# A decoder trunk on one core: seven more side steps in the second branch, an earlier and divided dt chain, and the added halves one pair of blocks per step

## Chip, core and metric

The kernel runs on one core of a Trainium2 chip, as one launch. The metric is the device time of one execution in microseconds (us), and a kernel's time is the median of its runs. The core has a matrix engine (TensorE; PE in the profile, PEld for its weight loads), a vector engine (VectorE, DVE), an engine for functions of single elements (ScalarE, ACT), a general engine (GpSimd, POOL) and SyncE (SP), whose queue issues all of this kernel's transfers.

## What is computed

One layer of a decoder, for 512 positions of width 1024, in float32. A normed input `u` is multiplied by one wide matrix `w_in`; its columns feed three mixers (windowed attention in three groups of six heads, causal pooling, a state space scan, SSD), whose outputs are gated, added and projected; a gated convolution network and two more norms follow.

```python
u = rmsnorm(x, ln1_g)
q, k, v, pool_in, z, xbc, dt_raw, gate_pre = jnp.split(u @ w_in, split_idx, axis=-1)
y_a = dilated_attention_mixer(q, k, v, rel_bias) @ w_a
y_b = pool_mixer(pool_in, pool_w, pool_scale) @ w_b
y_c = ssd_mixer(z, xbc, dt_raw, ...) @ w_c
gates = sigmoid(gate_pre + b_gate).reshape(b, s, 3, D_MODEL)
x = x + (gates[:, :, 0] * y_a + gates[:, :, 1] * y_b + gates[:, :, 2] * y_c) @ w_o
x = x + conv_ffn(rmsnorm(x, ln2_g), ...)
out = rmsnorm(x, final_g)
# inside ssd_mixer
dt = jax.nn.softplus(dt_raw + dt_bias)
A = -jnp.exp(a_log)
a_cs = jnp.cumsum(dt * A, ...)      # per chunk of 128 positions
```

The change lies in the stretch of the second branch (`w_b`), the first half of its gates and the products for `v` of the second and third attention groups.

## The kernel before, in words

**Products.** Each float32 operand is split into a high part and a low part (names ending in `h` and `l`), and a product is three products of the parts. `mm3` (L230) writes them: first high weights with high inputs, then high with low, then low with high. A chunk of 128 output columns over a depth of 1024 is 3 x 8 = 24 matmuls of 128x512 into one bank of PSUM, the matrix engine's result memory (`chunk_a`; tile `pa`).

**Jobs.** The program is a list of jobs; each takes one block of weights (256 columns, so two chunks, in `jobs_a`). While job n runs, `prepare` has already written the low part of job n+1 (`lows`, L211, VectorE), asks for the high part of job n+2 (`cast`, L191, ScalarE, in two halves, each at one of the next two steps) and issues the load of job n+3 (`fetch`, L179, SyncE). The engines' own orders are the orders in which the kernel's code emits instructions (a manual schedule for PE, ACT, DVE and POOL); each engine works through its queue in order. There are two raw buffers, three for high parts, two for low parts, four PSUM banks for chunks (`mm`) and four for everything else (`sm`).

**Steps.** Work beside the big products is put between them by `step()`. A step lets every generator in `running` go on to its next `yield`, then takes one item off `waiting`, starts it and moves it to `running`. In the second branch, the gates and the q and k products a step follows each chunk; in the v pair (`sevens`) one follows each product. Chunks of the last q and k jobs (`qk_jobs`, group 2) are already cut into two runs of 12 matmuls, with a step between.

**Attention items.** `attend(0)` puts twelve items (three pairs of heads, two banks of blocks, two heads) and one for statistics on `waiting`. An item computes scores `ps` for both heads of a pair if it is the first of them (L651), adds the bias (L658 to L665), takes the maximum (L661, L669) and the exponential (L672, ScalarE); two steps later it transposes the probabilities (`pt`, L678) and copies them to `sb` (L679, by VectorE for the even head and by ScalarE for the odd one); for the odd head, one step later still, come the products with v (`po`, L690), and after a pair's last bank their copy (L696, ScalarE).

**dt chain.** `ssd_prep` is one item of the same list, put in at place 5. It loads small vectors (first step), prepares dtx and an exponential (second), and in its third step runs 22 short instructions on VectorE one after another, a rational series for the logarithm (L845 to L855). Two steps later come four small matmuls (`pcs`, L859 to L862), then copies and exponentials, and one step on, four transposes (`pact`), two copies (`acst`, `east`) and their stores (`ad`, `ed`).

**Added halves.** The v columns of groups 1 and 2 are made with seven products in place of eight (`v_pair`, `sevens`), which take sums of quarters of the normed rows. The rows lie in eight blocks; `sums_of_u(p)` handles pair p of them. It adds high and low part of two blocks (`uf`, L388), next step forms four quarter sums `sa` and `sb` (L306 to L309), next step casts them (`sah`, `sbh`, ScalarE), next step subtracts (`sal`, `sbl`, L315 and L316, VectorE). The second product of `sevens` (the job `three`) reads `sbh` and `sbl` of all four pairs; the first (`one`) reads none. Beside the low part of their weights, `one`, `three` and `two` each form a difference of weight blocks on VectorE (L321).

In `program`, the four generators start ahead of the last job of the second branch, pairs 0 and 1 at its first step and pairs 2 and 3 one step later:

```python
yield Call(lambda: running.extend(after(p // 2, sums_of_u(p)) for p in range(4)))
```

Gate chunks are evacuated by a sigmoid (ScalarE, L1043) and multiplied into `yo` (VectorE, L1045). Sigmoid and exponential need different function tables on ScalarE (ACT_TABLE_LOAD).

Of the kernel before, what the change touches and what calls it, by code (L numbers as in the profile page):

```python
# [16 lines left out]
P = 128  # L17
# [66 lines left out]
def trunk(ctx: ExitStack, tc, out, x, rel_bias, ln1_g, w_in, b_gate, w_a, pool_w, pool_scale, w_b,  # L84
# [40 lines left out]
    waiting, running = [], []  # L125
# [19 lines left out]
    def step():  # L145
        flush()
        for it in list(running):
            try:
                next(it)
            except StopIteration:  # L150
                running.remove(it)
        if waiting:
            it = iter(waiting.pop(0))
            running.append(it)
            try:
                next(it)
            except StopIteration:
                running.remove(it)

    def after(n, it):  # L160
        for _ in range(n):
            yield
        yield from it
# [60 lines left out]
    def mm3(ps, wh, wl, xh, xl, ks, first=True, last=True, flip=False):  # L224

        n, total = 0, 3 * len(ks)
        for a, b in ((wh, xh), (wh, xl), (wl, xh)):
            for k in ks:
                l, r = (b(k), a(k)) if flip else (a(k), b(k))
                pe.matmul(ps, l, r, start=first and n == 0, stop=last and n == total - 1)  # L230
                n += 1

    def chunk_a(ps, ws, j, xh, xl, ks, lo=0, hi=S, k0=0):
        wh, wl = ws
        mm3(ps[:, lo:hi], lambda k: wh[:, k0 + k, j * P:(j + 1) * P],
            lambda k: wl[:, k0 + k, j * P:(j + 1) * P],
            lambda k: xh(k)[:, lo:hi], lambda k: xl(k)[:, lo:hi], ks)

    def jobs_a(w, c0, count, xh, xl, nk, evac, width=256):

        per = width // P
        for i in range(0, count, per):
            def body(ws, i=i):
                for j in range(per):
                    ps = MM("pa")
                    chunk_a(ps, ws, j, xh, xl, range(nk))
                    evac(i + j, ps)
                    if nk > 4 or j % 2:
                        step()
            yield Job([wsrc(w, 0, nk, c0 + i * P, c0 + i * P + width)], nk, width, body)  # L250
# [132 lines left out]
    def sums_of_u(p):  # L383

        f = []
        for k in (2 * p, 2 * p + 1):
            f.append(T("uf"))
            dve.tensor_tensor(f[-1], uh[:, k, :].bitcast(F32), ul[:, k, :].bitcast(F32), OP.add)  # L388
        yield
        yield from sums_of(*f, T("sah", F32R), T("sal", F32R),  # L390
                           lambda j, h, l: US.__setitem__((j, p), (h, l)))
# [210 lines left out]
    def qk_jobs(g):  # L602
        for i in range(3):
            def body(ws, i=i):
                for j, which in enumerate("qk"):
                    ps = MM("pqk")
                    if g == 2 and i >= 3 - MORE:

                        wh, wl = ws
                        for k0 in (0, 4):  # L610
                            mm3(ps, lambda k: wh[:, k, j * P:(j + 1) * P],
                                lambda k: wl[:, k, j * P:(j + 1) * P], uhk, ulk, range(k0, k0 + 4),
                                k0 == 0, k0 == 4)
                            if k0 == 0:
                                step()
                    else:
                        chunk_a(ps, ws, j, uhk, ulk, range(KD))
                    t = T(f"{which}{g}")
                    if which == "q":
                        act.mul(grouped(t, g), blocked(ps, g), 0.125)  # L620
                    else:
                        dve.tensor_copy(plain(t, g), perm(ps, g))
                    QK[which, g, i] = t
                    step()
            cq, ck = C_Q + 384 * g + i * P, C_K + 384 * g + i * P
            yield Job([wsrc(w_in, 0, KD, cq, cq + P), wsrc(w_in, 0, KD, ck, ck + P)], KD, 256, body)
# [131 lines left out]
    DP, YB = {}, {}  # L758
# [64 lines left out]
    def ssd_prep():  # L823

        f = lambda nme: cst.setdefault(nme, cpool.tile([P, n16], F32, name=nme))
        b16 = cpool.tile([P, 2, SH], F32, name="b16")
        for i, src in enumerate((ssd_dt_bias, ssd_a_log)):
            sp.dma_start(b16[:, i, :], src[0].partition_broadcast(P))

        dr, gr = T("dr"), T("gr")  # L830
        sp.dma_start(dr[:8, S - 2:], ssd_d[0].rearrange("(c h) -> c h", h=2))
        sp.dma_start(gr[:8, :P], ssd_norm_w[0].rearrange("(c p) -> c p", p=P))
        yield
        dve.tensor_copy(dr[:8, :P].rearrange("p (h d) -> p h d", h=2),
                        dr[:8, S - 2:].unsqueeze(2).to_broadcast([8, 2, DH]))
        dgc = cst["dgc"] = cpool.tile([P, 16], F32, name="dgc")
        v4 = lambda t: t.rearrange("p (a b) -> p a b", a=4)
        bc = lambda i: b16[:, i, :].unsqueeze(1).to_broadcast([P, 4, SH])
        xx, t, u, s, zz, dtv, a = (f(nme) for nme in ("dtx", "dtt", "dtu", "dts", "dtz", "dtv", "dta"))
        dve.tensor_tensor(v4(xx), dtr, bc(0), OP.add)  # L840
        dve.scalar_tensor_tensor(t, xx, -1.0, xx, OP.mult, OP.max)
        act.activation(t, t, AF.Exp, scale=-1.0)
        act.activation(b16[:, 1, :], b16[:, 1, :], AF.Exp)
        yield
        dve.tensor_scalar(u, t, 2.0, None, OP.add)  # L845
        dve.reciprocal(u, u)
        dve.tensor_mul(s, t, u)
        dve.tensor_mul(zz, s, s)
        dve.tensor_scalar(u, zz, 2.0 / 17, 2.0 / 15, OP.mult, OP.add)
        for d in (13, 11, 9, 7, 5, 3, 1):  # L850
            dve.tensor_mul(u, u, zz)
            dve.tensor_scalar(u, u, 2.0 / d, None, OP.add)
        dve.tensor_mul(u, u, s)
        dve.scalar_tensor_tensor(dtv, xx, 0.0, u, OP.max, OP.add)
        dve.scalar_tensor_tensor(v4(a), v4(dtv), -1.0, bc(1), OP.mult, OP.mult)  # L855
        yield
        yield
        ps = SM("pcs")
        pe.matmul(ps[:, :n16], tri, a, start=True, stop=True)  # L859
        pe.matmul(ps[:, n16:2 * n16], ones, a, start=True, stop=True)  # L860
        for i, r in enumerate((dr, gr)):
            pe.transpose(ps[:, 2 * n16 + 8 * i:2 * n16 + 8 * i + 8], r[:8, :P], eye[:8, :8])  # L862
        dve.tensor_copy(dgc, ps[:, 2 * n16:2 * n16 + 16])
        acs, tot, dec = (f(nme) for nme in ("acs", "tot", "dec"))
        dve.tensor_copy(acs, ps[:, :n16])
        dve.tensor_copy(tot, ps[:, n16:2 * n16])
        dve.tensor_tensor(dec, tot, acs, OP.subtract)
        act.activation(dec, dec, AF.Exp)
        act.activation(tot, tot, AF.Exp)
        yield  # L870
        pt = SM("pact")
        for c in range(4):
            pe.transpose(pt[:SH, c * P:(c + 1) * P], acs[:, c * SH:(c + 1) * SH], eye)
        at, et = T("acst"), T("east")
        dve.tensor_copy(at[:SH], pt[:SH])
        ad = cst["ad"] = dram.tile([SH, S], F32, name="ad")
        sp.dma_start(ad, at[:SH])
        act.activation(et[:SH], pt[:SH], AF.Exp)
        ed = cst["ed"] = dram.tile([SH, S], F32, name="ed")
        sp.dma_start(ed, et[:SH])  # L880
# [165 lines left out]

        return jobs_a(w_in, C_GATE + b * D + lo * P, hi - lo, uhk, ulk, KD, evac)

    def branch_jobs(b, w, parts, nk, last=False):
        def evac(m, ps):  # L1050
            if b == 1:
                MG[m] = T("yo")
                act.copy(MG[m], ps)
                return
            s = SG[b, m]
            dve.tensor_tensor(s, s, ps, OP.mult)
            (dve if last else pool).tensor_tensor(MG[m], MG[m], s, OP.add)
            if last:
                h, l = T("mgh", F32R), T("mgl", F32R)
                act.copy(h, MG[m])  # L1060
                dve.tensor_sub(l, MG[m], h.bitcast(F32))
                MH[m] = (h, l)

        return jobs_a(w, 0, 8, lambda k: parts[k][0], lambda k: parts[k][1], nk, evac,
                      width=256 if nk > 4 else 512)


    X1 = {}
# [319 lines left out]
    def program():  # L1388
# [3 lines left out]
        yield from qk_jobs(0)  # L1392
        yield from pool_out_job()
        yield Call(lambda: attend(0))
        yield Call(lambda: waiting.insert(5, ssd_prep()))
        for i, job in enumerate(branch_jobs(1, w_b, YB, 8)):
            if i == 3:
                yield Call(lambda: running.extend(after(p // 2, sums_of_u(p)) for p in range(4)))
            yield job
        load, pair = v_pair()  # L1400
        yield Call(load)
# [238 lines left out]
```

## Time and profile before

| what | value |
|---|---|
| runs of the kernel before | 1058.33, 1058.52, 1058.95 us; median 1058.52 |
| the profiled execution | 1059.66 us, of which 1057.6 us are the span from first to last instruction |
| mean granted clock of TensorE | 0.992 |
| busy: PE / PEld / DVE / ACT / POOL | 1039.9 / 866.4 / 642.2 / 477.7 / 137.9 us |
| second branch, four gate chunks (122.5 to 215.5 us) | 93.0 us: PE 87.2, DVE 54.7, ACT 46.5 busy, clock 0.93 |
| v pair (215.5 to 248.7 us) | 33.2 us: PE 33.2, DVE 28.5, ACT 18.4 busy, clock 1.00 |
| one chunk of 24 matmuls | about 5.4 us |

The profile names an instruction by engine, line, operation and tiles (out<-in), and a line can be that of a helper: L230 is `mm3`, whatever it works for. Times are from the span's start. "PEclk" is the share of full clock granted to TensorE, "[x <-Y]" the idle time before an instruction and what ended it, "x8" a merged run of eight.

### The profile page before, as it was taken

Reading aid. Unit: us, or ns where it says so; the run is one execution under the profiler, and the core shown is the slowest. Engines: PE = TensorE matmul, PEld = TensorE weight load, DVE = VectorE, ACT = ScalarE, POOL = GpSimd, SP = SyncE. Lnnn points to the kernel's source line nnn. Section 1 sums busy time; section 2 is a strip of 40 time slices with the busy share of each in tenths; the row PEclk is TensorE's granted clock in tenths of the full one; section 3 lists DMA queues with packets and bytes.
Section 4 is the critical chain, followed back from the end, with each engine's and each line's share of the span. In section 5 each row is a group of like instructions: output and inputs, shape, how many; then the busy total and the mean of one; then the engine's idle time right before and its main releaser. Section 6 shows DMA issues by size and latency. Waiting matters only on the chain.

```text
span 1057.6 us, 13100 instructions
## 1 busy us (share of the span) xinstructions
PE 1039.9 (98%) x5220; PEld 866.4 (82%) x5220; DVE 642.2 (61%) x867; ACT 477.7 (45%) x761; POOL 137.9 (13%) x118
## 2 busy tenths in 40 slices
PE   8999999799999999999999999999999999999997
PEld 8998888598888887788887888898888888878886
DVE  5553536776256556666577955766776656556545
ACT  6432542763384363566564423544444443433331
POOL 1770000000000001100135500001111111110110
PEclk9999999799999999999999999999999999999999
DMA  8454321125422346432244336643233232361332
GB/s 258 137 133 131 115 81 30 33 56 142 142 80 80 80 105 154 129 110 81 80 118 113 121 118 217 203 161 120 80 95 105 85 115 80 120 239 61 115 103 80
DMA packets 119787, 121.80 MB, mean 115 GB/s; under 512 B 5523, under 2 KB 101590, under 8 KB 119727
## 3 DMA queue, kind: packets, MB, share of 16 engines
q1 hardware_dynamic: 119727, 120.98, 37.5%
q8 instruction: 41, 0.67, 0.3%
q14 instruction: 19, 0.16, 0.0%
HBM read 115.07 MB, written 4.32 MB: 113 GB/s over the span
## 4 chain that ended last, share of the span: by engine, by line
PE 92%; DVE 3%; DMA 2%; ACT 2%; issue 0%; SPq 0%; DVEq 0%; ACTq 0%
PE pa L230 33%; PE pu L230 22%; PE pb L230 17%; PE pqk L230 9%; PE pa L1500 2%; PE p L230 2%; PE ps L651 1%; PE ppw L230 1%; PE po L690 1%; PE pt L678 1%; DMA al<-ad 1%; DMA raw<-in_w_in_dram 1%; DMA raw<-in_ffn_w_up_dram 1%; PE py L948 1%; PE pyo L954 1%; ACT wh L191 0%
## 5 line engine op out<-in xcount | busy, mean ns | idle before, releaser
L211 DVE TENSOR_TENSOR wl<-raw,wh 128x2048 fp32r<-128x2048 f32 (+3 forms) x95 | 218.5, 2300 | 89.3 <-ACT wh L191 53.6
L191 ACT CAST wh<-raw 128x1024 fp32r<-128x1024 f32 (+3 forms) x188 | 189.9, 1026 | 66.2 <-DVE raw L321 21.5
L230 PE MATMUL pa<-uh,wh 128*128 128x512 f32 x384 | 100.7, 405 | 0.0
L1158 DVE SCALAR_TENSOR_TENSOR hc<-pu,fcol,hc 128x510 f32<-128x510 f32 x88 | 65.8, 748 | 51.1 <-ACT hc L1155 49.5
L230 PE MATMUL pa<-ul,wh 128*128 128x512 f32 x384 | 95.2, 390 | 0.0
L230 PE MATMUL pa<-uh,wl 128*128 128x512 f32 x384 | 95.0, 390 | 0.0
L230 PEld LDWEIGHTS pa<-ul,wh 128*128 128x128 f32 x384 | 72.4, 189 | 15.4
L230 PEld LDWEIGHTS pa<-uh,wl 128*128 128x128 f32 x384 | 72.0, 188 | 15.3 <-DVE wl L211 0.3
L230 PEld LDWEIGHTS pa<-uh,wh 128*128 128x128 f32 x384 | 71.1, 191 | 16.2 <-issue 1.6
L230 PE MATMUL pu<-uh,wh 128*128 128x512 f32 (+1 forms) x352 | 83.7, 380 | 0.5 <-ACT uh L436 0.5
L230 PE MATMUL pu<-uh,wl 128*128 128x512 f32 (+1 forms) x352 | 83.5, 380 | 0.0
L230 PE MATMUL pu<-ul,wh 128*128 128x512 f32 (+1 forms) x352 | 83.5, 380 | 0.0
L230 PEld LDWEIGHTS pu<-uh,wh 128*128 128x128 f32 x352 | 64.1, 188 | 13.1 <-ACT uh L436 0.7
L230 PEld LDWEIGHTS pu<-ul,wh 128*128 128x128 f32 x352 | 64.2, 188 | 12.5
L230 PEld LDWEIGHTS pu<-uh,wl 128*128 128x128 f32 x352 | 64.2, 188 | 12.4
L1155 ACT ACTIVATE hc<-pu,fcol,fcol 128x512 f32<-128x512 f32 x40 | 31.2, 780 | 75.6 <-PE pu L230 75.3
L1163 POOL TENSOR_TENSOR hc<-hc 128x512 f32<-128x512 f32 x22 | 31.5, 1431 | 223.8 <-DVE hc L1158 169.3
L927 POOL TENSOR_TENSOR xd<-xc,dec 128x512 f32<-128x512 f32 x6 | 6.4, 1063 | 371.4 <-DVE xc L918 352.8
L672 ACT ACTIVATE sb<-sb,nm 128x128 f32<-128x128 f32 (+1 forms) x72 | 30.1, 419 | 29.3 <-DVE nm L669 18.1
L230 PE MATMUL pqk<-uh,wh 128*128 128x512 f32 x144 | 36.9, 394 | 0.0
L230 PE MATMUL pqk<-ul,wh 128*128 128x512 f32 x144 | 36.3, 390 | 0.0
L230 PE MATMUL pqk<-uh,wl 128*128 128x512 f32 x144 | 36.3, 390 | 0.0
(345 smaller groups left out, 1739.5 us busy)
## 6 DMA issues: line engine op xcount, KB each, us to landing
raw<-in_w_in_dram SPq DMA_DIRECT2D x25, 1024.0 KB
raw<-in_ffn_w_up_dram SPq DMA_DIRECT2D x22, 1024.0 KB
raw<-in_w_in_dram SPq DMA_DIRECT2D x20, 512.0 KB
raw<-in_ffn_w_down_dram SPq DMA_DIRECT2D x10, 1024.0 KB
raw<-in_w_o_dram SPq DMA_DIRECT2D x8, 1024.0 KB
raw<-in_w_b_dram SPq DMA_DIRECT2D x4, 1024.0 KB
al<-ad SPq DMA_DIRECT2D x16, 256.0 KB
raw<-in_w_c_dram SPq DMA_DIRECT2D x4, 1024.0 KB
```

The costliest lines, as they stand in the source:

```text
L191: act.copy(job.high[:, :, o], job.raw[:, :, o])
L211: (eng or dve).tensor_tensor(l[:, :, o], job.raw[:, :, o], h[:, :, o].bitcast(F32), OP.subtract)
L230: pe.matmul(ps, l, r, start=first and n == 0, stop=last and n == total - 1)
L651: pe.matmul(pss[i][:, o:o + w * P], q[r, n * P:(n + 1) * P], k[r, kb * P:(kb + w) * P], start=True, stop=True)
L672: act.activation(sb[:, off:off + w * P], sb[:, off:off + w * P], AF.Exp, bias=nm[:, n, h:h + 1], accum_out=ls[:, n, h:h + 1])
L678: pe.transpose(pt[:, o:o + P], sb[:, o:o + P], eye)
L690: pe.matmul(po[DH * hh:DH * hh + DH, n * P:(n + 1) * P], V[g, kb + i][:, (2 * c + hh) * DH:(2 * c + hh + 1) * DH], probs[2 * c + hh, nb][: ...
L948: pe.matmul(py[DH * i:DH * i + DH, j * P:(j + 1) * P], xc[:, o:o + DH], als[j // 2][:, lo:lo + P], start=True, stop=True)
L1155: act.activation(t, ps, AF.Identity, bias=ff["c1"][:, ff["b"] + m:ff["b"] + m + 1], scale=fw(2, m))
L1158: dve.scalar_tensor_tensor(t[:, sh:], ps[:, :S - sh], fw(k, m), t[:, sh:], OP.mult, OP.add)
L1163: pool.tensor_tensor(a, a, t, OP.mult)
L1500: pe.matmul(first[2 * n + j][:, lo:hi], a[:, k, j * P:(j + 1) * P], b[:, k, lo:hi], start=a is wh and b is uh and k == 0, stop=a is wl and ...
```

## The change

Three edits, no instruction of arithmetic added or taken away.

- Chunks 0 to 6 of the second branch are computed by a new `chunk_a2`: depth blocks 0 to 3 (12 matmuls), a step, depth blocks 4 to 7, into the same bank. `qk_jobs` calls the same function in place of its own copy of that code.
- `ssd_prep` goes into the list at place 3, two items further up, and a `yield` ahead of divisor 9 cuts the dt chain into two steps.
- The generators of the added halves start one pair per step (`after(p + 1, ...)`): pair 0 a step later than before, pairs 1, 2 and 3 each one step after the one before it.

```diff
+    def chunk_a2(ps, ws, j, xh, xl):
+
+        wh, wl = ws
+        for k0 in (0, 4):
+            mm3(ps, lambda k: wh[:, k, j * P:(j + 1) * P], lambda k: wl[:, k, j * P:(j + 1) * P],
+                xh, xl, range(k0, k0 + 4), k0 == 0, k0 == 4)
+            if k0 == 0:
+                step()
+
-    def jobs_a(w, c0, count, xh, xl, nk, evac, width=256):
+    def jobs_a(w, c0, count, xh, xl, nk, evac, width=256, more=()):
...
-                    chunk_a(ps, ws, j, xh, xl, range(nk))
+                    if i + j in more:
+                        chunk_a2(ps, ws, j, xh, xl)
+                    else:
+                        chunk_a(ps, ws, j, xh, xl, range(nk))
...
         for d in (13, 11, 9, 7, 5, 3, 1):
+            if d == 9:
+                yield
             dve.tensor_mul(u, u, zz)
...
-        yield Call(lambda: waiting.insert(5, ssd_prep()))
-        for i, job in enumerate(branch_jobs(1, w_b, YB, 8)):
+        yield Call(lambda: waiting.insert(3, ssd_prep()))
+        for i, job in enumerate(branch_jobs(1, w_b, YB, 8, more=range(7))):
             if i == 3:
-                yield Call(lambda: running.extend(after(p // 2, sums_of_u(p)) for p in range(4)))
+                yield Call(lambda: running.extend(after(p + 1, sums_of_u(p)) for p in range(4)))
             yield job
```

More of the change, by code (lines that the diff above doesn't have):

```diff
@@ L607, in body @@
                     if g == 2 and i >= 3 - MORE:
[L609 to L615, printed above, removed]
+                        chunk_a2(ps, ws, j, uhk, ulk)
                     else:
@@ L1047, in gate_jobs, with branch_jobs @@
         return jobs_a(w_in, C_GATE + b * D + lo * P, hi - lo, uhk, ulk, KD, evac)
-    def branch_jobs(b, w, parts, nk, last=False):
+    def branch_jobs(b, w, parts, nk, last=False, more=()):
         def evac(m, ps):
@@ L1064, in branch_jobs @@
         return jobs_a(w, 0, 8, lambda k: parts[k][0], lambda k: parts[k][1], nk, evac,
-                      width=256 if nk > 4 else 512)
+                      width=256 if nk > 4 else 512, more=more)
     X1 = {}
```

## The prediction, as it was made

> **What bounds the kernel now.** I read the page's busy times first, then its clock row, then TensorE's waits, then the timeline around the longest.
>
> ```profile
> PE 1039.9 (98%) x5220; PEld 866.4 (82%) x5220; DVE 642.2 (61%) x867; ACT 477.7 (45%) x761; POOL 137.9 (13%) x118
> ...
> PEclk9999999799999999999999999999999999999999
> ```
>
> TensorE is busy for 98% of the span, so only what stops or slows it can be won. The change moves work and leaves every matmul in place. One slice of the clock row is below 9: the eighth, 185 to 211 us. TensorE's waits between 100 and 260 us are two, both in that slice:
>
> ```profile
> PE po L690 <- ACT sb L679: 4.3, 1, 4.3
> PE ps L651 <- DVE tot L866: 1.5, 1, 1.5
> ```
>
> What the slice costs, the timeline of TensorE's weight loads tells, because the same train of work runs twice: the products of a head pair (po), three transposes (pt), a score block (ps), one chunk of 24 matmuls. First undisturbed, then in the bad place:
>
> ```profile
> 153.30 0.85 PEld L690 LDWEIGHTS po<-sb,v 128*64 128x64 f32 x16 [0.35 <-issue]
> ...
> 161.23 0.48 PEld L678 LDWEIGHTS pt<-eye,sb 128*128 128x128 f32 x3
> ```
> ```profile
> 187.31 0.19 PEld L690 LDWEIGHTS po<-sb,v 128*64 128x64 f32 x2
> 192.05 1.57 PEld L690 LDWEIGHTS po<-sb,v 128*64 128x64 f32 x14 [4.54 <-ACT sb L679]
> ...
> 206.68 0.53 PEld L873 LDWEIGHTS pact<-eye,acs 128*16 128x16 f32 x4
> ```
>
> 161.23 - 153.30 = 7.93 us against 206.68 - 187.31 = 19.37 us: **11.4 us are lost here**, 5.8 of them as waits, the rest because the clock is halved. The table by stretches shows that (columns: us, then PE, PEld, DVE, ACT, POOL busy, then PEclk):
>
> ```profile
> 186.35:189.76 3.41, 1.40 (x10) 0.99 (x8) 2.74 (x3) 3.38 (x6) 0.00 (x0) 1.00 0.17 18
> 189.76:193.17 3.41, 1.12 (x10) 1.12 (x12) 3.34 (x12) 3.39 (x6) 0.00 (x0) 0.50 0.60 215
> ...
> 200.00:203.41 3.41, 3.41 (x9) 2.64 (x8) 3.38 (x5) 2.34 (x7) 0.00 (x0) 0.50 0.00 0
> 203.41:206.82 3.41, 3.41 (x16) 2.72 (x15) 1.83 (x2) 0.84 (x1) 0.00 (x0) 1.00 0.00 0
> ```
>
> The clock falls to 0.50 at 189.8, some 2 us after the last matmul, and is back at 203.4, after a stretch in which TensorE worked throughout. Who is late? ScalarE copies the awaited tile last of a row:
>
> ```profile
> 185.73 0.51 ACT L672 ACTIVATE sb<-sb,nm 128x256 f32<-128x256 f32 x1 [9.39 <-DVE nm L661]
> ...
> 186.74 1.28 ACT L1043 ACT_TABLE_LOAD   x1
> ...
> 191.41 0.58 ACT L679 COPY sb<-pt 128x512 f32<-128x512 f32 x1
> ```
>
> It waited 9.39 us for VectorE, and then did a table load, a sigmoid, a cast and four sums casts ahead of the copy. VectorE was busy for 16.07 of the 17 us from 169 to 186: four uf (2.40 us), an attention block (1.33), the dt chain (22 instructions, 173.71 to 179.41 = 5.70), two sets of sums (2 x 1.47), four more uf (2.41).
>
> **The change, part by part.**
>
> *Side steps.* Chunks 0 to 6 of the second branch become 12 + 12 matmuls with a step between: the same 24 weight loads and matmuls, no new instruction. The fourteen attention and statistics items, the dt chain inserted among them, start one per step in order; with 15 steps instead of 8 before the gates, the attention is nearly over when they begin. In the order of the built program TensorE's breaks for them are 15 in both. A break that opens with po or ps costs a 0.35 us gap (0.25 behind the 384-wide matmuls): five and two before, seven and none after, so +0.2 us.
>
> Does the denser stretch stall? I laid the order out with the rows' durations (half a chunk 2.70, ps 1.06, four pt 0.55, po 1.02). A score block ends at 126.6; VectorE's add and maximum (1.33) follow its low part (to 126.9) and end at 128.2, ScalarE's exponentials (1.1) at 129.5; the transposes are due two steps on, at 132.0: 2.5 us to spare, the tightest of these chains. Per chunk TensorE now takes about 8.2 us, VectorE's share is two blocks 2.7, a copy 0.65, half a low part 1.14 = 4.5, ScalarE's the same size (exponentials 2.2, copies 1.3, cast 0.95). One place is even: at step 10 the third head pair's second score bank is free only after ScalarE's east (L878), which stands behind an evacuation and half a cast (0.48 + 0.95 + 0.59): 0.1 us late by my count, 0 to 0.3. Sigmoids no longer alternate with exponentials here, so the built order has 34 table loads for 42, eight of 1.28 us fewer on ScalarE; it does not set the end here, so I give them nothing of their own. The weight casts come half a chunk earlier; a w_b load issued at 114.95 has moved its megabyte by 120 us (the DMA row has 264 GB/s from 116 to 120), and the cast is due at 125.
>
> *dt chain.* It is split 2.53 + 3.17 us and put at steps 6 and 7. The block behind its second part is added by 151.3, TensorE refills that bank at 153.5. Hidden; without that cover each part would cost up to its length. Its two small loads now pass SP's queue (0.46 + 0.29 us) ahead of the two gate loads, and the ad and ed stores (0.34 + 0.33) ahead of the v pair's loads. SP stands waiting for low parts there (109.9 us in all), and the store's data come before the low part that the next load awaits: nothing.
>
> *Sums.* 8 uf, 16 quarter sums, 8 casts and 8 low parts stay; one pair starts per step, from the end of chunk 6. So they end later in the program: the last sbl is issued after the first v product, and the second product (three in `sevens`) reads it as its eighth weight load. **Here I find a new wait.** Let E be the end of the second gate chunk. VectorE's queue, by start-to-start times of these rows:
>
> ```profile
> 201.73 1.75 DVE L211 TENSOR_TENSOR wl<-raw,wh 128x1536 fp32r<-128x1536 f32 x1
> 203.51 1.76 DVE L321 TENSOR_TENSOR raw<-w,raw 128x1536 f32<-128x1536 f32 x1
> ...
> 207.82 0.69 DVE L1045 TENSOR_TENSOR yo<-yo,sg 128x512 f32<-128x512 f32 x1 [2.55 <-ACT sg L1043]
> 208.43 0.67 DVE L875 COPY acst<-pact 16x512 f32<-16x512 f32 x1
> 209.03 0.67 DVE L315 TENSOR_TENSOR sal<-sa,sah 128x512 fp32r<-128x512 f32 x1
> 209.63 0.67 DVE L316 TENSOR_TENSOR sbl<-sb,sbh 128x512 fp32r<-128x512 f32 x1
> ```
>
> The gate multiply starts 1.14 after its chunk's end (207.82 - 206.68). Then, in program order: three multiplies 3 x 0.61, four pairs of sal and sbl 4 x 1.20, two sets of sums 2 x 1.47, two uf 1.20, two low parts and two differences of 1536 columns 1.78 + 3 x 1.67 + 0.1. Sum 17.6, no gap among them: the last sbl is there at E + 18.8. TensorE needs two gate chunks (10.7), the first product (4.17) and seven loads (1.2): E + 16.1. It **waits 2.7 us** (2.2 to 3.3 with a few hundredths per instruction). Behind it are all later matmuls. The products after it have their operands: the next low part is ready at E + 20.5, wanted at E + 23.
>
> Does this wait halve the clock? None of 2.7 us is in the trace. Nearest below: 1.2 us near 12 us, clock 1.00. Nearest above: 4.3 us, halved, after a stretch of 3.41 us with 1.40 busy. The times of fall and return, 189.76 and 203.41, lie 4 x 3.41 apart, so I take fixed stretches of 3.41. A 2.7 us gap leaves one of them with 1.40 busy or less, that is 2.0 idle or more, in (0.7 + 2 x 0.7) / 3.41 = 6 of 10 positions (0.7 of them with the whole gap in one stretch, 0.7 at either edge). Then one full stretch runs at half speed and loses 3.41 / 2 = 1.7 us, up to 3.4 if it takes two. I take 1.7, nearest to the row that halved; bounds 0 and 3.4.
>
> The Trainium skill (TensorE: Matmul & The Clock Gate, Part 1) speaks of a free-running window of about 3.4 us and of half clock after at least one idle window. The spacing agrees with the trace. By its word "idle" a 2.7 us wait would never close the gate; the stretch from 186.35 closed it with 1.40 us busy, so here the measurement speaks against the strict reading.
>
> **Sum.** -11.4 + 0.2 + 0.1 + 2.7 + 1.7 = -6.7 us. The profiled execution took 1059.66 (span 1057.6 and 2.1 around it): 1053.0 by its own time. The runs' median, 1058.52, is 1.1 lower; there it is **1051.8 us**.
>
> **Rivals.** (a) The new wait without the clock: 1050.1. For it: the gap is shorter than a stretch; so no stretch is without work; the strict reading of the Trainium skill's page named above gives this case. (b) No new wait, the full gain: 1058.5 - 11.4 + 0.3 = 1047.4. Against it: VectorE's sum would have to be 2.7 / 17.6 = 15% too long, and its equal rows differ by 6% (1.67 to 1.78) at most. (c) A wait of the old kind in the branch, where queues are denser, with a halved stretch of its own: 1051.8 + 2.5 + 1.7 = 1056.0. For it: the even place above, and po again last in ScalarE's row. (d) Slower: each of the twelve score blocks reaches its transposes late. It decides from 2.5 us of extra delay per block on; beyond that each adds its excess, twelve times over. From 6.7 / 12 = 0.56 us of excess the gain is gone; at 0.9 the time is 1051.8 + 10.8 = 1062.6. For it: ScalarE and VectorE serve strictly in order, as the 9.39 us wait shows. Against it: each has nearly half of its time free there. (e) That the change does not do what it says: the built order shows the halves, the earlier chain and the one-pair sums, so only their effect is open.
>
> **Chances.** Forecast 46%, (a) 30%, (b) 12%, (c) 8%, (d) 4%. Forecast and (a) hold 76%, so the range takes in (b): 1047.2. Its upper end takes the dear ends of both unknowns, 3.3 and 3.4, and 0.2 more on the even place: 1051.8 + 0.6 + 1.7 + 0.2 = 1054.3. 0.2% (2.1 us) is about what a measurement of this kernel can tell from no change. Faster 0.93 (the first three and 5% of c), same 0.04, slower 0.03.
>
> **What would show it.** Right: no wait of po for sb in the branch and gates; clock 1.00 there; one TensorE wait of 2 to 3 us on sbl in the second v product, with a slice of clock below 1.00 after it. Wrong: a TensorE wait in the branch, the clock halved there, or no wait on sbl. If the wait exists and the clock stays, (a) holds. If VectorE is idle between the gate multiplies and the last sbl, my queue sum is wrong.

## The result and the profile after

| | before | after |
|---|---|---|
| runs beside each other on one chip, median | 1058.74 us (1058.33 to 1059.74) | 1052.12 us (1051.2 to 1053.23) |
| ratio, 95% interval | | 0.9937 (0.9919 to 0.9954) |
| profiled execution, span | 1059.66, 1057.6 us | 1052.9, 1050.8 us |
| mean granted clock | 0.992 | 0.997 |

Set against the 1058.52 us that the prediction started from, its 1051.8 us is a ratio of 0.9937. The busy times and the clock row of the page after, the two lines that were shown of before:

```profile
PE 1037.0 (99%) x5220; PEld 864.9 (82%) x5220; DVE 642.9 (61%) x867; ACT 467.4 (44%) x753; POOL 137.7 (13%) x118
...
PEclk9999999999999999999999999999999999999999
```

VectorE does the same 867 instructions, ScalarE eight fewer (the table loads, 8 x 1.28 us), and the eighth slice has its clock back. A slice is 26 us long, so it cannot show one halved stretch of 3.4 us; that has to be looked for in finer stretches. TensorE's waits between 100 and 260 us, after:

```profile
PE pb L230 <- DVE sbl L328: 2.2, 1, 2.2
```

The two waits of before (4.3 on `po`, 1.5 on `ps`) are gone and one on `sbl` has come. The timeline of VectorE and TensorE around it (the same two views as in the prediction; the columns are start, duration, instruction, and the idle time before it):

```profile
199.59 0.69 DVE L1052 TENSOR_TENSOR yo<-yo,sg 128x512 f32<-128x512 f32 x1 [2.72 <-ACT sg L1050]
...
214.29 1.75 DVE L333 TENSOR_TENSOR w<-w,w 128x1536 f32<-128x1536 f32 x1
215.96 0.69 DVE L327 TENSOR_TENSOR sal<-sa,sah 128x512 fp32r<-128x512 f32 x1
216.56 0.68 DVE L328 TENSOR_TENSOR sbl<-sb,sbh 128x512 fp32r<-128x512 f32 x1
```
```profile
214.43 0.69 PE L230 MATMUL pb<-wh,sbl 128*128 128x384 f32 x3
217.29 0.44 PE L230 MATMUL pb<-wh,sbl 128*128 128x384 f32 x1 [2.18 <-DVE sbl L328]
```

From the gate multiply at 199.59 to the last `sbl` at 216.56 VectorE has no gap, and TensorE, three of four `sbl` products done, stands from 215.1 to 217.29. The table by stretches (us, then PE, PEld, DVE, ACT, POOL busy, then PEclk) shows what that did to the clock:

```profile
214.40:217.81 3.41, 1.23 (x8) 0.91 (x7) 3.41 (x4) 1.47 (x3) 0.00 (x0) 1.00 0.00 0
217.81:221.22 3.41, 3.41 (x13) 3.41 (x12) 2.77 (x2) 0.48 (x1) 0.00 (x0) 0.50 0.00 0
221.22:224.64 3.42, 3.42 (x21) 3.42 (x20) 0.49 (x1) 2.47 (x4) 0.00 (x0) 1.00 0.00 0
```

One stretch has 1.23 us of work in it, the next runs at half clock, the third is whole again. That is the forecast, wait and clock both.

**Where the 6.8 us of the span come from.** Three matmuls mark the stretch that the change touches: the first of the second branch (`ybh`), the first of the v pair (`pb`), the first of the q and k products (`pqk`). Before, then after, from TensorE's timeline:

```profile
122.72 1.98 PE L230 MATMUL pa<-ybh,wh 128*128 128x512 f32 x8
...
215.48 0.97 PE L230 MATMUL pb<-wh,uh 128*128 128x384 f32 x4
...
248.83 2.01 PE L230 MATMUL pqk<-uh,wh 128*128 128x512 f32 x8
```
```profile
123.43 1.07 PE L230 MATMUL pa<-ybh,wh 128*128 128x512 f32 x4
...
209.55 0.87 PE L230 MATMUL pb<-wh,uh 128*128 128x384 f32 x4
...
242.72 2.01 PE L230 MATMUL pqk<-uh,wh 128*128 128x512 f32 x8
```

Branch and gates went from 92.76 to 86.12 us, the v pair from 33.35 to 33.17, the sum from 126.11 to 119.29: -6.82 us. What lies ahead of the first mark and behind the last differs by +0.71 and -0.69 between the two executions. These intervals inside a span carry the experiments, because they hold still where whole times of a kernel spread by 1 to 3 us.

### The profile page after: what moved, and what is told of

Its sections match the earlier page's. It is cut to its first block, busy times and chain, and to the rows that moved or that the text cites. A ratio compares the mean times of both kernels' runs of the same rounds, so it can differ in the third digit from the quotient of the medians.

```text
span 1050.8 us, 13095 instructions
## 1 busy us (share of the span) xinstructions
PE 1037.0 (99%) x5220; PEld 864.9 (82%) x5220; DVE 642.9 (61%) x867; ACT 467.4 (44%) x753; POOL 137.7 (13%) x118
## 4 chain that ended last, share of the span: by engine, by line
PE 94%; DVE 3%; DMA 1%; ACT 1%; issue 1%; POOL 0%; SPq 0%; DVEq 0%; ACTq 0%; POOLq 0%
PE pa L230 32%; PE pu L230 22%; PE pb L230 17%; PE pqk L230 9%; PE pa L1507 2%; PE p L230 2%; PE ps L656 1%; PE pu L1329 1%; PE po L695 1%; PE pt L683 1%; PE ppw L230 1%; DVE wl L211 1%; PE py L955 1%; DMA raw<-in_w_in_dram 1%; PE pyo L961 1%
## 5 line engine op out<-in xcount | busy, mean ns | idle before, releaser
L1050 ACT ACTIVATE sg<-pa,col 128x512 f32<-128x512 f32 x24 | 16.5, 687 | 51.8 <-PE pa L230 51.7
```

The source lines that it names most:

```text
L1050: act.activation(s, ps, AF.Sigmoid, bias=col[:, o:o + 1])
```

## The experiments

All on the same marks, one profiled execution each; times are medians of 4 to 6 runs (10 for the sums alone, 12 for one table), ratios to the kernel before on the same chip. "Waits" are TensorE's between 100 and 260 us, "halved" is the time there at half clock.

| run | median us | ratio (95%) | branch + gates | v pair | sum | waits | halved |
|---|---|---|---|---|---|---|---|
| before | | | 92.76 | 33.35 | 126.11 | po 4.3, ps 1.5 | 13.65 us |
| the change | 1052.12 | 0.9937 (0.9919, 0.9954) | 86.12 | 33.17 | 119.29 | sbl 2.2 | 3.4 |
| the change, once more | 1050.46 | 0.9918 (0.9905, 0.993) | 86.09 | 31.60 | 117.69 | sbl 2.2 | none |
| steps alone | 1048.94 | 0.9914 (0.9897, 0.993) | 87.05 | 29.14 | 116.19 | po 0.9 | none |
| dt alone | 1054.4 | 0.9968 (0.9955, 0.9981) | 89.66 | 33.34 | 123.00 | ps 3.6, po 1.0 | 6.8 |
| sums alone | 1058.81 | 0.9999 (0.9986, 1.0012) | 88.99 | 38.00 | 126.99 | ps 3.8, sbl 2.8 | 6.8 and 3.4 |
| steps and dt | 1048.22 | 0.9895 (0.9881, 0.9908) | 86.13 | 29.14 | 115.27 | none | none |
| steps and sums | 1052.27 | 0.9937 (0.9924, 0.995) | 87.06 | 31.62 | 118.68 | sbl 2.2, po 0.9 | none |
| sums a step earlier | 1047.47 | 0.9903 (0.9888, 0.9918) | 86.15 | 29.14 | 115.29 | none | none |
| wait shortened | 1048.93 | 0.9901 (0.9888, 0.9915) | 86.11 | 29.96 | 116.07 | sbl 0.5 | none |
| wait lengthened | 1055.16 | 0.9964 (0.995, 0.9977) | 86.13 | 36.88 | 123.01 | sbl 5.1 | 6.8 |
| before, one table | 1055.92 | 0.9973 (0.9965, 0.9982) | 90.27 | 33.34 | 123.61 | po 2.9, ps 0.7 | 10.2 |
| before, uf on GpSimd | 1053.91 | 0.9955 (0.9943, 0.9967) | 88.79 | 33.66 | 122.45 | ps 3.3, po 0.5 | 6.8 |
| before, both of these | 1051.04 | 0.993 (0.9917, 0.9943) | 83.95 | 33.35 | 117.30 | ps 2.0 | none |

Without side steps the v pair takes 33.3 us even undisturbed, because the last attention items still stand between its products; with them it takes 29.14.

Waits and clock together account for every row. Against the 115.28 us of the versions without a wait, the loss is the waits plus half of the work done at half clock: before, 5.8 + 9.85 / 2 = 10.7 of 10.83; one table, 3.6 + 9.23 / 2 = 8.2 of 8.33; sums alone, 6.6 + (6.77 + 3.40) / 2 = 11.7 of 11.71. No row is off by more than 0.6 us.

My theory: the train was lost to one queue through VectorE and ScalarE; the side steps spread it and win it back; the added halves, one pair per step, then bring a new wait, which counts in full, and a halved stretch of the clock on top. Rivals: ScalarE's table loads made the lost train; another part than the side steps won it; the wait on `sbl` costs nothing at the end.

### Which part wins

Steps alone (the change without the other two edits):

```diff
-            yield Call(lambda: waiting.insert(3, ssd_prep()))
+            yield Call(lambda: waiting.insert(5, ssd_prep()))
...
-                yield Call(lambda: running.extend(after(p + 1, sums_of_u(p)) for p in range(4)))
+                yield Call(lambda: running.extend(after(p // 2, sums_of_u(p)) for p in range(4)))
```

> Only the side steps; dt chain and added halves as before. If the side steps carry the gain and the one-pair sums bring the wait on sbl: no wait of po on sb, no wait on sbl (all sbl are issued before the gates end), clock 1.00 through the gates, 1047.2 to 1048.5 us, so faster than the whole change. If the undivided dt chain (5.7 us on VectorE) matters in the denser branch: a TensorE wait of 2 us or more on a score block's successors, 1050 to 1055 us.

Measured: 1048.94 us, 0.4 above the range. The first theory has no wait, and one small one is there:

```profile
PE po L695 <- ACT sb L684: 0.9, 1, 0.9
```

The undivided dt chain held VectorE until 158.4, ScalarE's exponentials waited 5.00 us for it, and the copy that `po` needs 0.9 us late. The side steps alone take 9.9 of 126.11 us out of the stretch, more than the whole change.

dt alone (kernel before, with the new place and the `yield`):

```diff
         for d in (13, 11, 9, 7, 5, 3, 1):
+            if d == 9:
+                yield
...
-        yield Call(lambda: waiting.insert(5, ssd_prep()))
+        yield Call(lambda: waiting.insert(3, ssd_prep()))
```

> Only the dt chain, two items further up and in two steps. If VectorE's backlog from 169 to 186 us is the cause, taking 5.7 us out of it brings the awaited copy forward by as much and the 4.3 us wait is gone; the attention still runs into the gates with exponentials and sigmoids in turn, so smaller waits may stay: 1048 to 1054 us. If the alternating table loads of ScalarE are the cause, they stay, and so does the time: 1057 to 1059 us.

Measured: 1054.4 us, 0.4 above the range of the one theory and below that of the other. The wait on `po` shrank to 1.0, and another took its place:

```profile
PE ps L651 <- ACT east L880: 3.6, 1, 3.6
PE po L690 <- ACT sb L679: 1.0, 1, 1.0
```

Sums alone (kernel before; not `p + 1`, but `p`, which starts pair 0 where it was):

```diff
-                yield Call(lambda: running.extend(after(p // 2, sums_of_u(p)) for p in range(4)))
+                yield Call(lambda: running.extend(after(p, sums_of_u(p)) for p in range(4)))
```

> Only the added halves, one pair per step, begun at the first step of the last branch job (a step earlier than in the change, since the second v product needs them in this kernel after fewer steps). If VectorE's backlog is the cause: 3.9 us of uf and sums go from ahead of the late maximum, the 4.3 us wait shrinks to 1 us or less, but the last sbl stands behind a low part and a difference: 1050 to 1056 us. If the table loads are the cause: 1057 to 1060 us.

A miss: 1058.81 us, no gain. The time is the one named for table loads as the cause, but the wait on `po` is gone with all table loads in place, so that cause is not what it shows. The next items in the same queue are as late:

```profile
PE ps L651 <- DVE tot L866: 3.8, 1, 3.8
PE pb L230 <- DVE sbl L316: 2.8, 1, 2.8
```

Its ten runs lie in two groups: five of 1056.36 to 1057.96 with a mean clock of 0.995 to 0.997, five of 1059.66 to 1060.87 with 0.992 or 0.993. So how much of the clock is lost differs from run to run of one program.

Steps and dt (the change with `p // 2` as before):

> The changed kernel with the added halves started as before (two pairs of blocks at the first step, two at the next): side steps and dt chain alone. My theory (the side steps win the lost train back; the dt chain, earlier and divided, takes away the 0.9 us wait that the side steps alone still had; the added halves one pair per step bring only the wait on sbl): no TensorE wait on sb in the branch and none on sbl, clock 1.00, 1047 to 1048.5. Rival (two pairs of added halves per step are a backlog of VectorE by themselves, which the one-pair start is there to remove): a TensorE wait of 1 to 4 us in the branch or the gates, 1049 to 1054.

Measured: 1048.22 us, no TensorE wait between 100 and 260 us. Two pairs per step make TensorE wait nowhere once the attention has gone by. Beside the steps, the dt edit is worth the 0.92 us between 116.19 and 115.27.

Steps and sums (the change with the dt chain as before):

> The changed kernel without the edit of the dt chain (one step, place 5): side steps and one pair of sums per step. My theory (the dt chain's edit is worth the 0.9 us wait that the side steps alone still had, the sums bring the wait on sbl): TensorE waits 0.9 us on ScalarE's sb in the branch and 2.2 us on sbl; 1050.5 to 1053.5, clock halved after the second or not. Rival (the dt chain's edit does nothing): 1050 to 1052, no wait in the branch. Rival (undivided, the chain meets a denser queue and costs TensorE more than 2 us): 1053.5 to 1056.

Measured: 1052.27 us, with the two waits of 0.9 and 2.2 together: 115.28 + 0.92 + 2.46 = 118.66 against 118.68 (the 2.46 us for the second wait is worked out below). The parts add.

### What the new wait costs

Sums a step earlier (the change with `after(p, ...)` in place of `after(p + 1, ...)`):

> The whole change, with the added halves begun one step earlier (after(p) for after(p + 1)): the last sal and sbl then stand ahead of a low part and a difference of 3.34 us in VectorE's queue. If the wait on sbl and the halved clock behind it are what the change gave back: no such wait, clock 1.00, 1047.2 to 1048.5 us in every run. If the loss comes from something else: 1051 to 1053 us as before.

Measured: 1047.47 us; of the four runs, two lie 0.4 below and 0.1 above the range that was given for every run (1046.8, 1048.6). No wait, clock 1.00 from 100 to 260 us. The marks stand at 122.19, 208.34 and 237.48, a stretch of 115.29 us, 4.0 less than the change.

Wait shortened (a difference of weight blocks goes behind the last low parts):

```diff
-        three.then = lambda: diff(W[0], W[1], W[0])
-        two.then = lambda: diff(W[1], W[1], one.raw)
+        def two_then():
+            diff(W[0], W[1], W[0])
+            diff(W[1], W[1], one.raw)
+
+        two.then = two_then
```

> The changed kernel, with one VectorE difference of 1536 columns (1.67 us) moved from ahead of the last two low parts of the sums to behind the low part that follows them. The last sbl then comes 1.67 us earlier, and TensorE's wait of 2.2 us on it should shrink to about 0.5 us. My theory (a wait counts in full, and the clock is halved only when much of one stretch of 3.41 us is idle): no halved stretch, 1048 to 1049, that is the version without any wait (1047.5) and 0.5 to 1. Rival (the wait on sbl is not what the change gave back; something else in the stretch is): about 1051 to 1053, as the change. Rival (any wait, however short, can halve a stretch): 1049 to 1051.

Measured: 1048.93 us, the wait 0.5 us as worked out (2.2 - 1.67), no halved stretch. The v pair takes 0.82 more than without a wait, 0.3 more than the idle time that the profile shows.

Wait lengthened (`again` is 4 for the last pair, else 0):

```diff
-        dve.tensor_sub(al, sa, ah.bitcast(F32))
+        for _ in range(1 + again):
+            dve.tensor_sub(al, sa, ah.bitcast(F32))
```

> The changed kernel, with the last sal computed four times more ahead of the last sbl (4 x 0.60 = 2.4 us of VectorE work, same values). My theory (VectorE's queue sets this wait, TensorE's loss grows one for one, and a gap of 4.6 us halves one stretch in every run): the wait is 4.6 us, the time 1054.5 to 1056, and the runs lie closer together than those of the change. Rival (the wait is hidden later, the end is set elsewhere): within 0.5 us of the change, 1051.5 to 1053. Rival (the longer gap halves two stretches or more): 1056.5 to 1059.

Measured: 1055.16 us, with runs nearly as far apart as the change's (1054.92 to 1056.66), not closer. The time lies in my range, but its parts do not, so that is partly luck. The wait is 5.1, not 4.6: VectorE took 3.51 us from the first `sal` to `sbl` (215.53 to 219.04), 2.9 more than the 0.60 of one, where 2.4 was reckoned. And two stretches are halved, as the second rival had it. The table by stretches:

```profile
214.80:218.20 3.40, 0.00 (x0) 0.00 (x0) 3.30 (x5) 0.66 (x1) 0.00 (x0) 0.99 0.00 0
218.20:221.60 3.40, 1.82 (x6) 1.82 (x7) 3.37 (x5) 0.00 (x0) 0.00 (x0) 0.50 0.00 0
221.60:225.00 3.40, 3.40 (x12) 3.40 (x11) 1.46 (x1) 0.48 (x1) 0.00 (x0) 0.50 0.00 0
225.00:228.40 3.40, 3.40 (x21) 3.40 (x21) 0.95 (x1) 2.94 (x5) 0.00 (x0) 1.00 0.00 0
```

The stretch with 1.82 us of work, at half clock, did not bring the full clock back; the full one behind it did. The v pair lost 36.88 - 29.14 = 7.74 us: 5.1 of wait, and 2.6 of clock, which is half of the work done at half speed, (1.82 + 3.40) / 2.

The change once more, unchanged:

> The changed kernel as it is, once more, for the spread of its runs and their mean granted clocks. My theory (the 2.2 us wait halves a stretch of 3.41 us or not, by where the stretches fall): two groups some 1.7 us apart, near 1051.2 and 1053, the slower one with a mean clock lower by about 1.7 / 1050 = 0.002. Rival (the clock is halved in every run, and the spread is of another cause): one group, or two with the same clock. Median 1051 to 1053 by both.

Measured: 1050.46 us, 0.5 below the range of both; the five runs spread from 1049.59 to 1051.62, not in two groups, and their mean clocks (0.997 to 0.999) do not sort them. But the profiled execution, set beside the first one, decides the point. Its wait is the same:

```profile
217.25 0.45 PE L230 MATMUL pb<-wh,sbl 128*128 128x384 f32 x1 [2.18 <-DVE sbl L328]
```

and the stretches behind it are at full clock:

```profile
215.68:219.09 3.41, 1.84 (x10) 1.85 (x11) 3.41 (x5) 0.63 (x2) 0.00 (x0) 1.00 0.00 0
219.09:222.50 3.41, 3.41 (x21) 3.41 (x21) 1.44 (x1) 1.94 (x4) 0.00 (x0) 1.00 0.00 0
...
1041.70:1045.11 3.41, 0.97 (x5) 0.46 (x3) 2.47 (x7) 0.93 (x3) 0.00 (x0) 1.00 0.42 154
1045.12:1048.53 3.41, 0.00 (x0) 0.00 (x0) 1.16 (x3) 0.00 (x0) 0.00 (x0) 0.50 0.41 154
```

Where the stretches lie is read from the clock's own changes. Before, the clock was half for four of them, 13.65 us, and then full for 849.92 us until its fall at the program's end; that is nearest to 249 stretches, of 3.4133 us each. In the change's first profiled execution it falls at 217.81, returns at 221.22 and falls once more at the program's end, at 1047.25; that is 243 stretches after 217.81. In this one its only fall within the span is at 1045.11, so 242 such stretches earlier a boundary stands at 219.09, and the next one before it at 215.68. The same idle time (215.07 to 217.25 here, 215.12 to 217.29 there) is cut in two by the boundary at 215.68 here, and its larger part lies in a stretch that keeps 1.84 us of work; there it lies whole in the stretch from 214.40 to 217.81, which keeps 1.23. In steps and sums a boundary cuts the same wait at 216.38, its two stretches keep 2.09 and 2.55 us, and the clock stays.

The v pair takes 31.60 here and 33.17 there: **1.57 us for one halved stretch**, and 31.60 - 29.14 = 2.46 for the wait itself, 0.28 more than its 2.18 us of idle time.

### What made the lost train

Before, one table (exponentials for the first four gate chunks):

```diff
-            act.activation(s, ps, AF.Sigmoid, bias=col[:, o:o + 1])
+            act.activation(s, ps, AF.Exp if b == 1 and lo == 0 else AF.Sigmoid, bias=col[:, o:o + 1])
```

> The kernel before, with exponentials in place of the sigmoids of its first four gate chunks, so that ScalarE needs no other table there (the values of these gates are wrong by that). Rival (ScalarE's table loads make the lost train; the side steps win because sigmoids no longer stand between exponentials): no wait on po, 1047 to 1050. My theory (VectorE's backlog makes ScalarE's row late by 9.39 us, one table load of 1.28 us ahead of the copy is the smaller part): a wait on po of about 3.0 us remains, the clock is still halved, 1055 to 1058.

Measured: 1055.92 us, a wait of 2.9 on `po`, the clock halved for 10.2 us. ScalarE's timeline:

```profile
185.41 0.51 ACT L672 ACTIVATE sb<-sb,nm 128x256 f32<-128x256 f32 x1 [9.40 <-DVE nm L661]
...
189.68 0.58 ACT L679 COPY sb<-pt 128x512 f32<-128x512 f32 x1
```

It still waits 9.40 us for VectorE. The table load was 1.4 of the 4.3, no more.

Before, `uf` on GpSimd:

```diff
-            dve.tensor_tensor(f[-1], uh[:, k, :].bitcast(F32), ul[:, k, :].bitcast(F32), OP.add)
+            pool.tensor_tensor(f[-1], uh[:, k, :].bitcast(F32), ul[:, k, :].bitcast(F32), OP.add)
```

> The kernel before, with the eight additions uf on GpSimd (idle between 100 and 260 us) in place of VectorE: 2.40 + 2.41 us fewer in VectorE's queue of 16 us, all else and all table loads as before. My theory (VectorE's backlog): ScalarE's row starts up to 4.8 us earlier, the 4.3 us wait on po is gone or under 1 us, no halved stretch there, 1048 to 1052; later table loads may still cost TensorE 1 to 4 us. Rival (table loads): the wait stays over 3 us, 1056 to 1059. Rival (GpSimd's additions take longer than a step, and VectorE then waits for them in order): a wait on po or ps for VectorE, 1055 to 1062.

Measured: 1053.91 us, above the range that I gave. The wait on `po` fell to 0.5 with all table loads in place:

```profile
181.88 0.51 ACT L672 ACTIVATE sb<-sb,nm 128x256 f32<-128x256 f32 x1 [6.04 <-DVE nm L661]
...
187.58 0.58 ACT L679 COPY sb<-pt 128x512 f32<-128x512 f32 x1
```

The copy comes 3.83 us earlier than before (191.41), which is the wait that went; it is not 4.81, since one VectorE instruction ahead of it, `dtt`, took 0.98 us longer (see the last section). But `ps` for `tot` grew to 3.3, behind a gate multiply whose sigmoid stands after two table loads.

Before, both of these edits:

> The kernel before with both of the last two edits: the eight additions uf on GpSimd, and exponentials in place of the sigmoids of the first four gate chunks (these gates' values are wrong by that). Alone, the first left waits of 0.5 on po and 3.3 on ps, the second 2.9 on po and 0.7 on ps. My theory (the lost train is one queue through VectorE and ScalarE; 2.4 us of additions and two table loads of 1.28 us stand in it one behind the other): 0.5 and 3.3 shrink by one and two table loads, so none on po and 0.7 on ps, no halved stretch, 1047 to 1050. Rival (two separate causes that do not add): a wait of 2 us or more and a halved stretch remain, 1051 to 1054.

Measured: 1051.04 us. No wait on `po`, no halved stretch, the two edits together more than either; but 2.0 us remain on `ps`, not 0.7, so the sizes do not simply add, and the median lies above my range. The trace shows what stands ahead of the awaited `tot` (191.06): a gate multiply that waited 1.43 us for its sigmoid. The sigmoid stands behind exponentials (188.64) that waited 1.93 us for VectorE's maximum, and the maximum behind eight quarter sums (184.74 to 187.67) that follow one another with no gap. So what is left is VectorE's share of the row; no run takes the quarter sums out.

## Why the prediction was right

- **The lost train, -11.4, and +0.3 for gaps and the even place.** Versions without any wait take 115.28 us for the stretch of 126.11: -10.83 against -11.1. The 11.4 was split into 5.8 of waits and the rest for the clock, 5.6; half of the work done at half clock is 4.9. The cause stands too. Relieving VectorE alone took the wait on `po` from 4.3 to 0.5, taking away the table loads alone to 2.9. But the forecast said too little of the second half: sums alone, dt alone and `uf` on GpSimd took that wait to nothing, 1.0 and 0.5, and got another of 3.3 to 3.8 on the next item. Of the single edits only the side steps ended the row. With them the last score block (171.66) comes 14 us ahead of the gates (185.85). They also bring the eight table loads fewer, which the forecast put at nothing of their own, and no run takes the two apart within the side steps; in the kernel before, the table loads were 1.4 of the 4.3. What both relieve does not add: without the table loads the stretch is 2.50 us shorter, with `uf` on GpSimd 3.66, with both 8.81.
- **The denser stretch.** No TensorE wait in the branch. The tightest chain, the first score block, by ScalarE's timeline:

```profile
128.94 0.51 ACT L677 ACTIVATE sb<-sb,nm 128x256 f32<-128x256 f32 x1 [1.43 <-DVE nm L674]
...
129.45 0.50 ACT L677 ACTIVATE sb<-sb,nm 128x256 f32<-128x256 f32 x1
```

  It ends at 129.95, and the transposes begin at 132.65: 2.7 us to spare, 2.5 forecast. ScalarE's longest wait for VectorE's maximum is 2.9 us in the branch, where it was 9.4. The even place (`east` ahead of `ps`) shows no wait, 0.1 forecast.
- **dt chain: nothing.** Beside the sums and steps it hides, as forecast; without it the steps have a 0.9 us wait, a gain that the forecast did not see because it reckoned the three edits together.
- **The new wait, 2.7: measured 2.2**, in its place. VectorE's sum gave E + 18.8; with E = 198.67 (the start of the next chunk) TensorE went on at 217.29, E + 18.6; the gate multiply began 0.92 after E, not 1.14. TensorE wanted it at E + 16.44, not 16.1: two gate chunks took 10.88 and the seven loads 1.38. It counts in full: 2.46 us longer with it, 0.82 with the shortened one.
- **The clock, 1.7: 1.57 when it falls**, and it falls in some executions only: in one of two profiled ones of the same program, with the same gap of 2.18 us. The 6 in 10 was worked out for 2.7 us; by the same sum a 2.2 us gap leaves 2.0 idle in one stretch in (1.2 + 2 x 0.2) / 3.41, that is in 5 of 10 positions. So forecast and rival (a), 1050.1, are both this kernel, and the medians of the two sets of runs, 1052.12 and 1050.46, are nearest to the one and to the other. That the set taken for the result lay nearer to the forecast than to (a) is luck. The Trainium skill (TensorE: Matmul & The Clock Gate, Part 1) says that the window runs free and that its phase varies from run to run; these two executions agree, with boundaries at 217.81 and 219.09. Its condition of one idle window does not: stretches with 1.40 and 1.23 us of work were followed by half clock.
- **The other rivals.** (b), no wait, is what starting the sums a step earlier gives, 1047.47; the change as made has the wait. (c) and (d) did not occur; (c) would have been right for the side steps without the dt edit, at 0.9 us and without the clock.

The two versions without any wait are the change without its last step of delay (sums from `after(p, ...)`), 0.9903 (0.9888 to 0.9918), and without the edit of the sums, 0.9895 (0.9881 to 0.9908). Their intervals do not part them, nor from the shortened wait (0.9901) and the side steps alone (0.9914).

## What to carry to other kernels

Where TensorE waited on a row of small work served in order, spreading the row over more places between the products won more than thinning one entry, which handed the wait to the next. Work moved later has a reader: sum the queue of its engine up to that reader's need before moving it, here 18.8 us against 16.1 from the same mark, and stop one step sooner. The wait of two microseconds cost its length in each execution and half of a clock stretch in one of two, so compare intervals inside the span, and more than one profiled execution.

## What the runs showed of the hardware

- In each of these traces the clock changes only at whole multiples of 3.4133 us from its other changes, and where these boundaries lie in the span differs between executions. A gap of 2.18 us halved the next stretch in one execution and none in another; a gap of 5.1 us halved two.
- Over the stretches of all fourteen traces, each of the eight at full clock that were followed by half clock ahead of the program's end held 0 to 1.41 us of TensorE work; none that held 1.66 us or more was followed by half clock. At half clock, stretches with 1.12 to 3.36 us of work (2.83 in the kernel before, 3.36 in the sums alone) did not bring the full clock back, and those with 3.39 or more did. The ends of matmuls are modelled, so these borders are rough.
- VectorE's `dtt` (L841, 128x64) took 1.21 us in the run with `uf` on GpSimd, from 169.81 to 171.02, while GpSimd worked on its additions (168.27 to 170.94); before it took 0.23. The run with both edits shows it again: 1.21 us, to 171.00, with GpSimd's additions to 170.92. The three VectorE instructions just ahead of it, in the same overlap, took 0.69, 0.22 and 0.21, as before within 0.02. The Trainium skill (Trainium Architecture — The Big Picture, What this means for kernel authors) says that these two engines share a port pair under an exclusive lock; the end of `dtt` fits that, why the three ahead of it were not held up stays open, and no run here separates the two.
